# Differential attention in a hybrid layer: the turned output copied out of PSUM by VectorE and squared later by ScalarE, the last-but-one query group's small transfers on GpSimd's queue

## The chip, the cores and the metric

The kernel runs on one core of a Trainium2 chip. The metric is device time in microseconds (us) of one execution; lower is better. Before the change three runs took 2862.43, 2862.50 and 2864.21 us (median 2862.5 us).

## The reference, cut to what matters

One layer of a hybrid backbone: a combined input projection, differential attention with four heads beside a Fourier mix, an output projection of both, and a squared-ReLU MLP. The attention is where the change lies. Each head has two score maps (m = 0, 1), and their softmaxes are subtracted; each head's output is then normalised over its 128 values:

```python
def one_block(qblk):
    s = jnp.einsum('bqhmd,bkhmd->bhmqk', qblk, k).astype(jnp.float32) * scale
    p = jax.nn.softmax(s, axis=-1)
    a = p[:, :, 0] - lam * p[:, :, 1]
    return jnp.einsum('bhqk,bkhe->bqhe', a.astype(v.dtype), v)

def merge(attn, four, subln_g, lam_init, w_out):
    b, n = attn.shape[:2]
    a = rms_norm(attn, subln_g) * (1.0 - lam_init)
    return jnp.concatenate([a.reshape(b, n, ATTN_WIDTH), four], axis=-1) @ w_out
```

There are 2048 latent queries against 2560 keys (512 cached, 2048 latent), and 256 prompt queries against the prompt's own 256 keys.

## The kernel before

**Engines.** PE is TensorE, PEld its weight load, DVE VectorE, ACT ScalarE, POOL GpSimd, SP SyncE. Each works through its own instructions in the order in which they were written; an instruction that waits for another engine or a DMA holds up what is behind it.

**Stages.** Up to 517 us run the projections and the Fourier mix, which ends with four stores of ys to the array four by GpSimd's queue (L830). From 517 to 1250 us comes attention, then the out-projection, then the MLP, which TensorE fills to the end.

**Attention.** Each of four heads has eight groups of 256 queries (class Group), taken one after the other, and one prompt group. A group's steps are methods: fill (TensorE: scores S of 128 queries and 512 keys into a PSUM bank, two products, L1081), rowmax and comb (VectorE: the row's maximum, L1086 and L1089), exp (ScalarE: L1105, into P0 for m = 0 and P1 for m = 1, with the row sums), combine (VectorE sums, L1110 and L1111; GpSimd scales P1 and adds it to P0, L1112 to L1121), tr (TensorE turns P0 into pt, L1136), ah and al (ScalarE copies pt as the high part, VectorE takes the remainder, L1143 and L1148), mul (TensorE: values times probabilities into po, L95 to L97 for the split blocks, L1162 for blocks 4 and 14, which are kept whole in the tile af).

**The group's output.** po is one PSUM bank for all groups. Its columns 0 to 255 take the product; o1 copies them to oT (ScalarE, L1173), o2 turns oT with TensorE into po's columns 256 to 511 (L1177), o4 squares these with a sum over each row (ScalarE, two ACTIVATE into the scratch tile osq, L1183), o5 turns the sums into factors (GpSimd, L1186 and pow at L92), o6 stores the factors (DMA rs, L1194), o7 loads them back spread over the partitions (DMA rb, L1199), o8 multiplies oT by them (GpSimd, L1204), and o9 stores the result (DMA att, L1208). place says which queue o6, o7 and o9 use: SyncE's, or GpSimd's for the last group of the last head ("last", group 7). The one before it, group 6 of the last head, is "drain".

**What sets the order.** Every step is entered with a hand-written time by add(t, fn), in units of u = 1.04, the steps are sorted by these times and written out in that order. The last group's steps from o4 on are put aside (LASTO) and run inside the out-projection, the first two behind its first six products, the others behind its first twelve.

**The step into the out-projection.** The out-projection takes token tiles s0, s1 and so on. w_split makes high and low parts of the weights (woh on ScalarE, wol on VectorE, L1561 to L1565), mix those of the mixed activations (mh and ml on VectorE, L1588 and L1589, from mT), out_mm multiplies (L95 to L97), out_post adds to the residual (L1607, L1608), x_norm and finish feed the MLP. mix_load brings mT from att and four by SyncE's queue (L1581, L1582). In attention's pools tiles are laid out one behind the other in SBUF in the order of the pools: a_t (small tiles, ah, al, af, P1, and the output's tiles oT, osq, oss), then a_p (P0). They lie on memory that the stage before has given back.

Of the kernel before, what the change touches and what calls it, by code (L numbers as in the profile page):

```python
# [11 lines left out]
F32 = mybir.dt.float32  # L12
F32R = mybir.dt.float32r
AF = mybir.ActivationFunctionType
# [5 lines left out]
P = 128  # L20
# [21 lines left out]
def body(tc, a, out):  # L42
    nc = tc.nc
    ctx = ExitStack()
    with ctx:
# [944 lines left out]
        with ExitStack() as c3_:  # L990
# [4 lines left out]
            at = c3_.enter_context(tc.tile_pool(name="a_t", bufs=2, reuse_waits="tile"))  # L995
# [44 lines left out]
            class Group:  # L1040
# [97 lines left out]

                def ah(self, kb):
                    full = kb in self.hd.vf  # L1140
                    t = at.tile([P, 512], F32 if full else F32R, tag="af" if full else "ah", name=f"ah{self.nm}_{kb}", bufs=2 if full else 4)

                    (nc.vector.tensor_copy if self.drain and kb == FULL[0] else nc.scalar.copy)(t, self.pt[kb])  # L1143
                    self.A[kb] = [t]
# [30 lines left out]
                def o2(self):  # L1175
                    for j in range(2):
                        nc.tensor.transpose(self.po[:, 256 + j * P:256 + j * P + P], self.oT[:, j * P:j * P + P], ident)  # L1177

                def o4(self):
                    osq = self.op.tile([P, P], F32, tag="osq", name=f"osq{self.nm}", bufs=1)  # L1180
                    self.oss = self.op.tile([P, 4], F32, tag="oss", name=f"oss{self.nm}")
                    for j in range(2):
                        nc.scalar.activation(osq, self.po[:, 256 + j * P:256 + j * P + P], AF.Square, accum_out=self.oss[:, j:j + 1])  # L1183

                def o5(self):
                    nc.gpsimd.tensor_add(self.oss[:, 0:2], self.oss[:, 0:2], self.s0e)  # L1186
                    pow_mhalf(self.oss[:, 2:4], self.oss[:, 0:2], 2)

                def place(self):
                    return nc.gpsimd if self.last else nc.sync, self.hd.tok0 // 2 + self.g  # L1190

                def o6(self):
                    q, n = self.place()
# [16 lines left out]
            class Prompt(Group):  # L1210
# [39 lines left out]
                def mul(self):  # L1250

                    (ah, al), V = self.A[0], self.hd.V
                    for t in range(2):
                        c = slice(t * 256, t * 256 + 256)
                        for n, (l, r) in enumerate(((0, ah), (1, ah), (0, al))):
                            nc.tensor.matmul(PRO()[:, 256:512], V[:, t, l, :], r[:, c], start=False, stop=(t == 1 and n == 2), skip_group_check=True)
# [23 lines left out]
            def add(t, fn, *args):  # L1280
                ev.append((t, len(ev), fn, args))
# [20 lines left out]
            for h in range(H):  # L1302
                hd, hp = Head(0, h), Head(1, h)
                base = h * 32 * T
                add(base - 18 * T + 0.7 if h else -3.04 * T, hd.load_k)
                add(base - 14 * T + 0.7 if h else 0.9 * T, hd.load_v)
                e = 4 * T * (h == H - 1)
                add(base + 2 * T - e + 0.7, hp.load_k)
                add(base + 2 * T - e + 0.71, hp.load_v)
                gp = Prompt(hp, 0)  # L1310
                G = [base + (AVS + 4 * g) * T for g in range(8)]
                add(G[1] - 3 * T - e, gp.qload)
                for j in range(2):
                    for m in range(2):
                        for t, fn in ((0.4, gp.scores), (0.85, gp.rowmax), (2.7, gp.exp)):
                            add(G[1 + 2 * j + m] - e + t * u, fn, j, m)
                    add(G[2 + 2 * j] - e + 8 * u, gp.combine, j)
                for t, fn, *args in ((0.25, gp.tr, 0), (0.9, gp.ah), (1.4, gp.al), (17.0, gp.mul), (20.85, gp.o1), (24.45, gp.oq),
                                     (25.3, gp.o2), (26.0, gp.o5), (26.05, gp.opow), (29.5, gp.o6), (34.0, gp.o7),
                                     (40.2, gp.o8), (43.0, gp.o9)):  # L1320
                    add(G[5] - e + t * u, fn, *args)
                for g in range(hd.ng):
                    gr = Group(hd, g)
                    add(base - (4 if h or g > 1 else 3) * T + 0.6 * u if base else -3.03 * T, gr.qload)
                    for st in range(4):
                        j, m = divmod(st, 2)
                        t0 = base + st * T
                        for b in range(hd.nbk):
                            add(t0 - T + (0.76 + 0.66 * b) * u, gr.fill, j, m, b)
                            add(t0 - T + (1.26 + 0.66 * b) * u, gr.rowmax, j, m, b)  # L1330
                            add(t0 + 0.66 * b * u, gr.exp, j, m, b)
                        add(t0 - 0.45 * u, gr.comb, j, m)
                        if m:
                            add(t0 + (4.5 if gr.last and j else 5.9) * u, gr.combine, j)
                            if gr.last and j:
                                add(t0 + T + 5.3 * u, gr.combine_v, j)
                    kbs = list(range(0, hd.nkt, 2))
                    for q in range(4):
                        w = base + (AVS + q) * T
                        if q % 2 == 0:  # L1340
                            order = [kbs.pop(0) for _ in range(2)]
                            tr_t, ah_t, al_t = [0.7, 2.2], [3.3, 3.8], [4.6, 5.2]
                        else:
                            order = [kbs.pop(0) for _ in range(3)]
                            tr_t, ah_t, al_t = [0.7, 2.2, 3.86], [3.3, 3.8, 4.4], [None, 4.6, 5.2]
                        for n, kb in enumerate(order):
                            add(w + tr_t[n] * u, gr.tr, kb)
                            add(w + (2.0 if gr.drain and kb == FULL[0] else ah_t[n]) * u, gr.ah, kb)
                            if al_t[n]:
                                add(w + al_t[n] * u, gr.al, kb)  # L1350
                            add(w + T + (3.9 + 0.01 * n) * u, gr.mul, kb)
                            if q == 3 and not n:
                                add(w + 3.95 * u, gr.mul_part, kb)
                    w = base + (AVS + 5) * T + 1.0 * u
                    for t, fn in ((0, gr.o1), (0.4, gr.o2), (6.9, gr.o4), (9.2, gr.o5), (11.8, gr.o6), (16.3, gr.o7), (23.4, gr.o8), (26.0, gr.o9)):
                        if gr.last and t > 1:
                            LASTO.append(fn)
                        else:
                            add(w + t * u, fn)
                    base += 4 * T  # L1360
# [357 lines left out]
        with c5r, ExitStack() as c5:  # L1718
# [157 lines left out]
            with tc.manual_schedule():  # L1876
                for n, (q, p) in enumerate(ITEMS):
# [22 lines left out]
                    fn, args = FINISH.get(n, (None, ()))  # L1900
# [66 lines left out]
        with ExitStack() as c6:  # L1967
# [62 lines left out]
            with tc.manual_schedule():  # L2030
                pend, NM, loaded, KS = None, 7 * 24, 4, []
                for i in range(7):
                    for b in range(3):
                        ps = [pp.tile([P, 512], F32, tag="ps", name=f"ps{i}_{b}_{j}", bufs=6) for j in range(3)]
                        for k in range(16):
# [19 lines left out]
                            if (i, b) == (6, 2) and 9 <= k < 12:  # L2055

                                j = k - 9
# [14 lines left out]
                for j in range(3):  # L2072
                    t = 6 + j
# [70 lines left out]
```

## Time and profile before

| | us |
|---|---|
| median of 3 runs | 2862.5 |
| the profiled execution | 2864.23 |
| its span, first to last instruction | 2862.4 |
| PE busy | 2829.3 (99%) |
| DVE busy | 1978.0 (69%) |
| ACT busy | 1534.8 (54%) |
| POOL busy | 1075.4 (38%) |

The page's chain of work that ended last gives PE 54% of the span by name and DVE 1%. In rows of instructions the columns are start, duration, engine, line, operation, output and inputs, shapes and count, and in brackets the idle time ahead of it on its engine and what ended it. In rows of waits they are the total, the count and the longest.

### The profile page before, as it was taken

How to read it: one execution, taken by the hardware profiler on the slowest of the kernel's cores; microseconds unless marked ns; L12 is line 12 of the kernel's file. 1: busy time of each engine (PE TensorE's matmuls, PEld its weight loads, DVE VectorE, ACT ScalarE, POOL GpSimd, SP SyncE). 2: the span in 40 equal slices, each digit the busy share in tenths (PEclk: the TensorE clock that was granted, in tenths of full speed). 3: DMA queues.
4: the chain of work that ended last, by engine and by line, in shares of the span. 5: the costliest groups of instructions: out<-in, count | busy, mean ns of one | idle time of the engine just before them, and what ended most of it. 6: DMA issues, size and time to landing. Idle time of an engine off the chain costs nothing.

```text
span 2862.4 us, 42998 instructions
## 1 busy us (share of the span) xinstructions
PE 2829.3 (99%) x15029; PEld 2453.4 (86%) x15029; DVE 1978.0 (69%) x3325; ACT 1534.8 (54%) x3479; POOL 1075.4 (38%) x887
## 2 busy tenths in 40 slices
PE   8999999999999999999999999999999999999999
PEld 5888888688888888878889999999998888888887
DVE  7777786888888888864477777778775354345554
ACT  4333332798988989853356565556555332333221
POOL 1221223789999899942223333333332000000000
PEclk9999999999999999999999999999999999999999
DMA  7777767432222322246767676667747464445653
GB/s 284 219 209 204 234 203 253 153 105 54 78 74 53 112 62 75 50 120 210 247 221 232 221 247 229 220 220 238 233 168 256 147 202 136 137 143 185 208 203 111
DMA packets 404795, 497.69 MB, mean 174 GB/s; under 512 B 31539, under 2 KB 320672, under 8 KB 401506
## 3 DMA queue, kind: packets, MB, share of 16 engines
q1 hardware_dynamic: 399088, 484.35, 53.5%
q0 software_dynamic: 1936, 7.41, 0.8%
q10 hardware_dynamic: 3554, 3.17, 0.4%
q8 instruction: 119, 1.95, 0.3%
q14 instruction: 98, 0.80, 0.1%
HBM read 317.30 MB, written 179.62 MB: 174 GB/s over the span
## 4 chain that ended last, share of the span: by engine, by line
PE 54%; DVE 1%; DMA 0%; issue 0%; ACT 0%; POOL 0%; DVEq 0%; SPq 0%
PE ps L95 8%; PE ps L96 8%; PE ps L97 8%; PE pB L1761 2%; PE pB L1759 2%; PE pB L1760 2%; PE pA L1759 2%; PE pA L1761 2%; PE pA L1760 2%; PE pC L1761 2%; PE pC L1759 2%; PE pC L1760 2%; PE po L97 2%; PE po L96 2%; PE po L95 2%; PE pD L1759 1%
## 5 line engine op out<-in xcount | busy, mean ns | idle before, releaser
L1086 DVE TENSOR_REDUCE mxs<-Ss 128x1 f32<-128x512 f32 x636 | 405.4, 686 | 98.5 <-PE Ss L1081 91.2
L1436 DVE TENSOR_TENSOR sl<-sr,sh 128x768 fp32r<-128x768 f32 x168 | 161.8, 964 | 331.6 <-ACT sh L1435 331.1
L1121 POOL TENSOR_TENSOR P0s<-P0s,P1s 128x1024 f32<-128x1024 f32 (+2 forms) x128 | 378.5, 2957 | 10.7
L1435 ACT CAST sh<-sr 128x768 fp32r<-128x768 f32 x168 | 140.6, 838 | 418.3 <-PE ps L96 418.3
L1801 POOL TENSOR_TENSOR gs<-g,g 128x384 f32<-128x384 f32 x48 | 69.8, 1453 | 469.3 <-ACT g L1771 426.4
L1105 ACT ACTIVATE P1s<-Ss,mxs 128x512 f32<-128x512 f32 x318 | 215.2, 694 | 38.8 <-DVE mxs L1089 35.4
L95 PE MATMUL pj<-wh,hh 128*128 128x512 f32 x576 | 228.2, 396 | 2.0 <-DVE hh L556 2.0
L95 PE MATMUL ps<-thT,sh 128*128 128x512 f32 x585 | 227.6, 389 | 0.0
L96 PE MATMUL ps<-tlT,sh 128*128 128x512 f32 x585 | 227.6, 389 | 0.0
L97 PE MATMUL ps<-thT,sl 128*128 128x512 f32 x585 | 227.6, 389 | 0.0
L96 PE MATMUL pj<-wl,hh 128*128 128x512 f32 x576 | 227.0, 394 | 0.3 <-DVE wl L517 0.3
L97 PE MATMUL pj<-wh,hl 128*128 128x512 f32 x576 | 225.4, 392 | 0.0
L1105 ACT ACTIVATE P0s<-Ss,mxs 128x512 f32<-128x512 f32 x318 | 214.4, 691 | 4.9 <-DVE mxs L1089 4.0
L1136 PE MATMUL pts<-ident,P0s 128*128 128x128 f32 x1280 | 192.5, 274 | 4.5 <-DVE als L1148 1.8
L1081 PE MATMUL Ss<-KS0s,Qs 128*128 128x512 f32 x636 | 190.6, 420 | 0.4 <-ACT P1s L1105 0.4
L1081 PE MATMUL Ss<-KS1s,Qs 128*128 128x512 f32 x636 | 189.1, 422 | 1.5 <-ACT P0s L1105 1.1
L1136 PEld LDWEIGHTS pts<-ident,P0s 128*128 128x128 f32 x1280 | 152.5, 141 | 35.7 <-issue 4.6
L1770 ACT ACTIVATE g<-uz 128x384 f32<-128x384 f32 x144 | 75.7, 526 | 200.1 <-DVE uz L1793 174.0
L1120 POOL TENSOR_SCALAR P1s<-P1s,tots 128x1024 f32<-128x1024 f32 (+2 forms) x128 | 171.6, 1340 | 5.8
L1148 DVE TENSOR_TENSOR als<-pts,ahs 128x512 fp32r<-128x512 f32 x256 | 163.7, 681 | 9.4 <-ACT ahs L1143 9.3
L95 PE MATMUL ps<-ophT,sh 128*128 128x512 f32 x423 | 164.7, 389 | 1.1 <-DVE uz L1793 1.1
L1143 ACT CAST ahs<-pts 128x512 fp32r<-128x512 f32 x256 | 146.8, 604 | 34.1 <-PE pts L1136 34.1
(534 smaller groups left out, 8021.0 us busy)
## 6 DMA issues: line engine op xcount, KB each, us to landing
sr<-sd SPq DMA_DIRECT2D x84, 768.0 KB, 4.4
a<-in_w SPq DMA_DIRECT2D x184, 256.0 KB, 3.6
sd<-gs SPq DMA_DIRECT2D x192, 192.0 KB, 2.0
sd<-g SPq DMA_DIRECT2D x144, 192.0 KB, 4.1
wm<-in_w_mod SPq DMA_DIRECT2D x32, 512.0 KB, 5.3
Qs<-qd SPq DMA_DIRECT2D x32, 512.0 KB, 5.3
b<-in_w SPq DMA_DIRECT2D x64, 256.0 KB, 5.0
b<-tsum SPq DMA_DIRECT2D x64, 256.0 KB, 4.7
```

The source lines that it names most:

```text
L95: nc.tensor.matmul(ps, lh, rh, start=first, stop=False)
L96: nc.tensor.matmul(ps, lh, rl, start=False, stop=False)
L97: nc.tensor.matmul(ps, ll, rh, start=False, stop=last)
L1081: nc.tensor.matmul(S[:, :w], self.Q[:, x, m, j * P:j * P + P], self.hd.KS[m][:, b * 512:b * 512 + w], start=(x == 0), stop=(x == 1))
L1086: nc.vector.tensor_reduce(self.mx[j][:, m, b:b + 1], self.S[j, m, b], axis=AX.X, op=ALU.max)
L1105: nc.scalar.activation(dst, S, AF.Exp, bias=self.mx[j][:, m, 6:7], accum_out=self.sm[j][:, m, b:b + 1])
L1120: nc.gpsimd.tensor_scalar(p, p, tot[:, 3:4], 0.0, op0=ALU.mult, op1=ALU.add)
L1121: nc.gpsimd.tensor_add(d, d, p)
L1136: nc.tensor.transpose(pt[:, c:c + P], self.p0[j][:, (kb + t) * P:(kb + t + 1) * P], ident)
L1759: nc.tensor.matmul(ps, wh[:, c], hh[:, k, :], start=first and k == 0, stop=False, skip_group_check=True)
L1760: nc.tensor.matmul(ps, wh[:, c], hl[:, k, :], start=False, stop=False, skip_group_check=True)
L1761: nc.tensor.matmul(ps, wl[:, c], hh[:, k, :], start=False, stop=k == 3, skip_group_check=True)
```

## The change

1. A new step o3 copies the turned output, 128x256, from po to a new SBUF tile o on VectorE, at 4.25 u behind o1 (0.75 u for the last group). 2. o4 squares o in place instead of reading po, and goes from 6.9 u to 8.5 u; the scratch tile osq (128 wide) is gone, o is 256 wide. 3. af has one buffer instead of two. 4. The last-but-one group's o6, o7 and o9 go to GpSimd's queue.

```diff
-   t = at.tile([P, 512], F32 if full else F32R, tag="af" if full else "ah", name=f"ah{self.nm}_{kb}", bufs=2 if full else 4)
+   t = at.tile([P, 512], F32 if full else F32R, tag="af" if full else "ah", name=f"ah{self.nm}_{kb}", bufs=1 if full else 4)
...
+   def o3(self):
+       self.o = self.op.tile([P, 256], F32, tag="o", name=f"o{self.nm}", bufs=1)
+       nc.vector.tensor_copy(self.o, self.po[:, 256:512])
+
    def o4(self):
-       osq = self.op.tile([P, P], F32, tag="osq", name=f"osq{self.nm}", bufs=1)
        self.oss = self.op.tile([P, 4], F32, tag="oss", name=f"oss{self.nm}")
        for j in range(2):
-           nc.scalar.activation(osq, self.po[:, 256 + j * P:256 + j * P + P], AF.Square, accum_out=self.oss[:, j:j + 1])
+           o = self.o[:, j * P:j * P + P]
+           nc.scalar.activation(o, o, AF.Square, accum_out=self.oss[:, j:j + 1])
...
-       return nc.gpsimd if self.last else nc.sync, self.hd.tok0 // 2 + self.g
+       return nc.gpsimd if self.last or self.drain else nc.sync, self.hd.tok0 // 2 + self.g
...
-   for t, fn in ((0, gr.o1), (0.4, gr.o2), (6.9, gr.o4), (9.2, gr.o5), (11.8, gr.o6), (16.3, gr.o7), (23.4, gr.o8), (26.0, gr.o9)):
+   for t, fn in ((0, gr.o1), (0.4, gr.o2), (0.75 if gr.last else 4.25, gr.o3), (8.5, gr.o4), (9.2, gr.o5), (11.8, gr.o6), (16.3, gr.o7), (23.4, gr.o8), (26.0, gr.o9)):
```

**Place 1, the start of attention.** ScalarE's first exponentials, in the brackets what each waits for (a name without DMA is an engine, DMASW0 to 7 are the counters that GpSimd's DMAs raise in turn); before:

```order
L811 COPY abl_0_5199<-pabl_0_5196 128x130 [waits PE_49]
L811 COPY abl_1_5204<-pabl_1_5201 128x130 [waits PE_49,Activation_49]
L760 COPY yu<-py 128x129 [waits PE_49] x2
L1105 ACTIVATE P0s_0_0_5289,sms_0_0_5266<-Ss_0_0_0_0_5268,mxs_0_0_5265 128x512 [waits DVE_49,Pool_49]
L1105 ACTIVATE P0s_0_0_5289,sms_0_0_5266<-Ss_0_0_0_1_5272,mxs_0_0_5265 128x512
```

and now:

```order
L811 COPY abl_0_5199<-pabl_0_5196 128x130 [waits PE_49]
L811 COPY abl_1_5204<-pabl_1_5201 128x130 [waits PE_49,Activation_49]
L760 COPY yu<-py 128x129 [waits PE_49] x2
L1105 ACTIVATE P0s_0_0_5289,sms_0_0_5266<-Ss_0_0_0_0_5268,mxs_0_0_5265 128x512 [waits DMASW0_49,DVE_49,Pool_49]
L1105 ACTIVATE P0s_0_0_5289,sms_0_0_5266<-Ss_0_0_0_1_5272,mxs_0_0_5265 128x512
```

The first exponential has got a wait for DMASW0. GpSimd's last DMAs ahead of it are the stores of ys, in both kernels; each waits for the counter that it will raise:

```order
L779 TENSOR_TENSOR ys_4700<-yu 128x256
L830 DMA four<-ys_4697 128x2048 [waits DMASW5_49,DVE_49]
L830 DMA four<-ys_4698 128x2048 [waits DMASW6_49,DVE_49]
L830 DMA four<-ys_4699 128x2048 [waits DMASW7_49,DVE_49]
L830 DMA four<-ys_4700 128x2048 [waits DMASW0_49,DVE_49,Pool_49]
```

The count that the exponential waits for is the one that the fourth of these, ys_4700, raises when it has landed.

**Place 2, a group in the middle of attention.** ScalarE, group 3 of the first head (P0s and P1s are group 6's probabilities, ahs_4 group 4's), before:

```order
L1105 ACTIVATE P0s_6_0_6803,sms_6_0_6736<-Ss_6_0_0_4_6774,mxs_6_0_6735 128x512
L1183 ACTIVATE osqs_3_6848,osss_3_6849<-po 128x128 [waits DMAHW6_49,PE_49]
L1183 ACTIVATE osqs_3_6848,osss_3_6849<-po 128x128 [waits Activation_49]
L1143 CAST ahs_4_10_6853<-pts_4_10_6811 128x512 [waits PE_49]
L1143 CAST ahs_4_12_6858<-pts_4_12_6838 128x512 [waits PE_49]
```

and now:

```order
L1105 ACTIVATE P0s_6_0_6806,sms_6_0_6739<-Ss_6_0_0_4_6777,mxs_6_0_6738 128x512
L1143 CAST ahs_4_10_6854<-pts_4_10_6816 128x512 [waits PE_49,Activation_49]
L1143 CAST ahs_4_12_6859<-pts_4_12_6843 128x512 [waits PE_49,Activation_49]
L1187 ACTIVATE os_3_6810,osss_3_6876<-os_3_6810 128x128 [waits DMAHW6_49,DVE_49]
L1187 ACTIVATE os_3_6810,osss_3_6876<-os_3_6810 128x128
```

The two squares have gone behind the two copies and wait for VectorE. VectorE has the copy between the remainders and the sums:

```order
L1148 TENSOR_TENSOR als_4_6_6804<-pts_4_6_6759,ahs_4_6_6780 128x512 [waits Activation_49]
L1148 TENSOR_TENSOR als_4_8_6808<-pts_4_8_6782,ahs_4_8_6800 128x512 [waits Activation_49]
L1181 COPY os_3_6810<-po 128x256 [waits PE_49]
L1110 TENSOR_REDUCE tots_5_1_6596<-sms_5_1_6595 128x2 [waits Pool_49]
L1111 RECIPROCAL tots_5_1_6596<-tots_5_1_6596 128x1 [waits DVE_49]
L1086 TENSOR_REDUCE mxs_6_0_6738<-Ss_6_0_1_0_6821 128x1 [waits PE_49]
```

TensorE's order is the same in both; its first product of group 4, `L1162 MATMUL po<-ahs_4_4`, waits for VectorE where it waited for ScalarE.

**Place 3, the end of attention.** VectorE's last remainders and the out-projection's first splits, before:

```order
L1148 TENSOR_TENSOR als_7_16_14805<-pts_7_16_14775,ahs_7_16_14783 128x512 [waits Activation_49]
L1148 TENSOR_TENSOR als_7_18_14807<-pts_7_18_14785,ahs_7_18_14803 128x512 [waits Activation_49]
L1562 SCALAR_TENSOR_TENSOR wol_0_14890<-wout_13384,cols,woh_0_14882 128x512 [waits DMAHW6_49,Activation_49,Pool_49]
L1588 CAST mh_14911<-wout_13386 128x1024 [waits DMAHW2_49,DMAHW3_49,DMASW4_49,DMAHW6_49,DMASW3_49,DMAHW7_49,DMASW2_49,DMASW1_49]
L1589 TENSOR_TENSOR ml_14912<-wout_13386,mh_14911 128x1024 [waits DMAHW3_49,DVE_49]
```

and now (os_7 is the last group's copy, the lines are 4 higher):

```order
L1148 TENSOR_TENSOR als_7_16_14836<-pts_7_16_14806,ahs_7_16_14814 128x512 [waits DVE_49,Activation_49]
L1148 TENSOR_TENSOR als_7_18_14838<-pts_7_18_14816,ahs_7_18_14834 128x512 [waits DVE_49,Activation_49]
L1181 COPY os_7_14860<-po 128x256 [waits PE_49,Activation_49]
L1566 SCALAR_TENSOR_TENSOR wol_0_14923<-wout_13409,cols,woh_0_14915 128x512 [waits DMAHW6_49,Pool_49]
L1592 CAST mh_14944<-wout_13411 128x1024 [waits DMAHW2_49,DMAHW3_49,DMASW4_49,DMAHW6_49,DMASW3_49,DMAHW7_49,DMASW2_49,DMASW1_49]
L1593 TENSOR_TENSOR ml_14945<-wout_13411,mh_14944 128x1024 [waits DMAHW3_49,DVE_49]
```

The copy stands ahead of the three. GpSimd, the last two groups, now:

```order
L1198 DMA rs_84<-osss_6_14792 128x2 [waits DMASW1_49,Pool_49]
L1203 DMA rbs_6_14840<-rs_84 128x256 [waits DMASW2_49,DMASW1_49]
L1208 TENSOR_TENSOR oTs_6_14724<-oTs_6_14724,rbs_6_14840 128x256 [waits DMASW2_49,PE_49]
L1212 DMA att_79<-oTs_6_14724 128x256 [waits DMASW3_49,Pool_49]
L1190 TENSOR_TENSOR osss_7_14961<-osss_7_14961,s0es_7_14028 128x2 [waits Activation_49]
L92 TENSOR_TENSOR osss_7_14961<-osss_7_14961,mhalf 128x2 [waits Pool_49]
L1198 DMA rs_84<-osss_7_14961 128x2 [waits DMASW4_49,Pool_49]
L1203 DMA rbs_7_14981<-rs_84 128x256 [waits DMASW4_49]
L1208 TENSOR_TENSOR oTs_7_14856<-oTs_7_14856,rbs_7_14981 128x256 [waits DMASW5_49,PE_49]
```

The first, second and fourth rows stood on SyncE before, between the store of group 5's att and the load of mT.

## The prediction, as put on record

> **What bounds the kernel now.** I read the page's busy times first.
>
> ```profile
> PE 2829.3 (99%) x15029; PEld 2453.4 (86%) x15029; DVE 1978.0 (69%) x3325; ACT 1534.8 (54%) x3479; POOL 1075.4 (38%) x887
> ```
>
> TensorE is busy for 99% of the span, so an edit pays or costs only what it adds to or takes from TensorE's few stops. The change touches the attention stage alone (about 517 to 1250 us) and the step from it into the out-projection, so the second view is the table of waits from 560 to 1250 us.
>
> ```profile
> PEld Ss L1081 <- ACT P0s L1105: 14.9, 43, 0.5
> PEld po L1177 <- ACT oTs L1173: 12.0, 28, 0.7
> PEld po L1162 <- ACT osqs L1183: 10.1, 31, 0.3
> PEld Ss L1081 <- ACT P1s L1105: 5.2, 25, 0.2
> ```
>
> The third row is the one that the new copy addresses: 31 times the first value product of a group waits until ScalarE has squared the turned output of the group before, since both use the one PSUM tile po. PEld is only the weight load, though, which runs ahead of the products; 10.1 us is not yet TensorE's loss. The instruction rows tell what is. The first group has nothing to wait for, a later one has:
>
> ```profile
> 557.93 1.18 PE L1081 MATMUL Ss<-KS1s,Qs 128*128 128x512 f32 x4
> 558.94 1.03 PE L1162 MATMUL po<-ahs,vf4s 128*128 128x256 f32 x4
> 559.61 0.47 PE L95 MATMUL po<-ahs,Vs 128*128 128x256 f32 x1
> ...
> 715.27 1.17 PE L1081 MATMUL Ss<-KS1s,Qs 128*128 128x512 f32 x4
> 716.35 1.13 PE L1162 MATMUL po<-ahs,vf4s 128*128 128x256 f32 x4
> 717.13 0.47 PE L95 MATMUL po<-ahs,Vs 128*128 128x256 f32 x1
> ```
>
> From the four score products to the first L95 it is 559.61 − 557.93 = 1.68 us without the wait and 717.13 − 715.27 = 1.86 us with it. TensorE loses 0.18 us a group, about half of the row's 0.33 (10.1 / 31).
>
> **Term A, the copy and the later squares: −4.5 us.** If the wait went everywhere, 31 x 0.18 = 5.6 us would be won. What replaces it is VectorE's copy of 128x256 out of PSUM. The trace has no such copy; two rows lie on either side, a VectorE reduction that reads as much PSUM, and ScalarE's copy of that shape:
>
> ```profile
> L1225 DVE TENSOR_REDUCE tlp<-po x16: 424/424/425, 567.0 to 1149.5; 128x1 f32<-128x256 f32 x16
> ...
> 707.89 0.37 ACT L1173 COPY oTs<-po 128x256 f32<-128x256 f32 x1
> ```
>
> I take 0.42, VectorE's own. In the order it stands behind two remainders (als) and ahead of the sums, so in the group above here:
>
> ```profile
> 712.07 1.28 DVE L1148 TENSOR_TENSOR als<-pts,ahs 128x512 fp32r<-128x512 f32 x2
> 713.45 0.16 DVE L1111 RECIPROCAL tots<-tots 128x1 f32<-128x1 f32 x1
> 714.02 3.29 DVE L1086 TENSOR_REDUCE mxs<-Ss 128x1 f32<-128x512 f32 x5 [0.41 <-PE Ss L1081]
> ...
> 715.93 0.28 ACT L1183 ACTIVATE osqs<-po 128x128 f32<-128x128 f32 x1
> 716.10 0.20 ACT L1183 ACTIVATION_READ_ACCUMULATOR osqs<-po 128x1 f32 x1
> 717.60 0.69 ACT L1105 ACTIVATE P1s<-Ss,mxs 128x512 f32<-128x512 f32 x1 [0.34 <-DVE mxs L1089]
> ...
> 723.20 0.19 POOL L1186 TENSOR_TENSOR osss<-osss,s0es 128x2 f32<-128x2 f32 x1
> ```
>
> The copy runs from 713.35 to about 713.8, 2.5 us before the squares end now (716.30), so po is free in time and the wait goes. Its cover is the 0.41 us in which VectorE waits for scores: 0.42 fits in it almost exactly. What doesn't fit delays the row maxima, which then run without a gap, and with them the exponentials that already wait 0.34 for them; those free the banks that TensorE fills (the Ss rows above, 0.2 to 0.35 a time). Without that cover 30 groups would give back up to 0.18 each, and A would be 0. I charge 0.6 in all for it, and 0.5 at the last-but-one group, whose copy has remainders ahead of it longer than the squares took: 5.6 − 0.6 − 0.5 = 4.5. Bounds: 0 to −5.6. The squares (0.28 each) stay on ScalarE; from SBUF the trace has none, and I take the same length: were they twice as long, ScalarE would lose 0.6 us a group against the 0.34 that it waits there, which is the second rival's case. Moved behind two copies of probabilities they end about a microsecond later, at 717.4, and GpSimd comes to them at 723.20 only. One af buffer fewer is free: the product that uses it ends at 717.5 (716.35 + 1.13), and the next block's copy stands behind the exponentials that begin at 717.60.
>
> **Term B, the start of attention: +12.0 us.** Taking one af tile out and making o wider shortens the pool a_t by 2 − 0.5 = 1.5 KB a partition, and all that lies behind it moves down. The order of instructions shows what that does: the very first exponential, which before waits for VectorE and GpSimd, now waits for DMASW0 as well, the fourth of GpSimd's stores of the Fourier part (ys), whose tile lies where the probabilities now begin. When does that store land?
>
> ```profile
> 518.09 0.53 POOL L830 DMA_DIRECT2D four<-ys  x1 [0.35 <-issue]
> ...
> DMA to landing us min/median/max: 8.6/11.1/14.7
> ```
>
> ```profile
> 527.00:533.00 6.00, 5.70 (x18) 2.59 (x18) 5.57 (x14) 5.75 (x17) 4.61 (x5) 1.00 0.99 405
> 533.00:539.00 6.00, 5.72 (x18) 2.38 (x16) 5.56 (x13) 5.67 (x19) 5.74 (x5) 1.00 0.04 16
> ```
>
> The fourth store is issued at 518.09. In the windows (columns: PE, PEld, DVE, ACT and POOL busy, granted clock, share of the DMA engines) the DMA engines are full until about 533 and then empty, so the longest landing is the last one's: 518.09 + 14.7 = 532.8. Now the start as it is:
>
> ```profile
> 520.74 0.69 ACT L1105 ACTIVATE P0s<-Ss,mxs 128x512 f32<-128x512 f32 x1 [4.04 <-DVE mxs L1089]
> 521.57 1.40 PE L1081 MATMUL Ss<-KS1s,Qs 128*128 128x512 f32 x4 [1.10 <-ACT P0s L1105]
> 531.13 0.69 ACT L1105 ACTIVATE P1s<-po,mxs 128x512 f32<-128x512 f32 x1 [0.26 <-DVE mxs L1089]
> ```
>
> The first exponential runs at 520.74. TensorE has by then filled every bank and waits for it (1.10). From there to 545 ScalarE goes without a pause but for short ones like the 0.26 at 531.13, so it sets the pace and all behind it moves with it: 532.8 − 520.74 = 12.0. Two such pauses could be made up by maxima taken meanwhile (11.5). Were the fourth store as quick as the quickest, 518.09 + 8.6 = 526.7, it would be 6.0. Nothing hides any of it: there is no other work that TensorE could do there.
>
> By the Trainium skill (TensorE: Matmul & The Clock Gate, What's actually happening) an idle window of about 3.4 us halves TensorE's clock, and 12 us of idling would have TensorE refill the banks at half pace. This trace has that clock in one of the rows of the next part (0.50). ScalarE then has eight full banks to work off, so by that rule I'd add an estimated 0 to 1 us; I add nothing.
>
> **Term C, the step into the out-projection: −1.5 us.** Three DMAs of the last-but-one group go from SyncE's queue to GpSimd's, and the last group's copy stands on VectorE ahead of the weights' first split.
>
> ```profile
> 1245.40 1.32 DVE L1562 SCALAR_TENSOR_TENSOR wol<-wout,cols,woh 128x512 fp32r<-128x512 f32 x1
> 1247.36 1.23 DVE L1589 TENSOR_TENSOR ml<-wout,mh 128x1024 fp32r<-128x1024 f32 x1
> 1257.70 0.69 DVE L1588 CAST mh<-mT 128x1024 fp32r<-128x1024 f32 x1 [4.71 <-DMA mT<-att]
> ...
> 1248.01 0.44 PE L1177 MATMUL po<-ident,oTs 128*128 128x128 f32 x2 [0.46 <-ACT oTs L1173]
> 1258.54 0.47 PE L95 MATMUL po<-woh,mh 128*128 128x512 f32 x1 [4.39 <-DVE mh L1588]
> 1259.78 0.80 PE L97 MATMUL po<-woh,ml 128*128 128x512 f32 x1 [0.54 <-DVE ml L1589]
> ...
> 1246.20 0.32 SPq L1208 DMA_DIRECT2D att<-oTs  x1
> 1251.38 0.43 SPq L1581 DMA_DIRECT2D mT<-att  x1
> ...
> 1259.23:1262.64 3.41, 2.87 (x8) 2.29 (x8) 3.41 (x6) 0.00 (x0) 0.16 (x1) 0.50 1.02 351
> ```
>
> Now TensorE stops for 4.39 and 0.54 us and then runs 3.41 us at half clock, 1.7 lost: 6.6 in all. The cause is the load of mT, issued only at 1251.38 behind two DMAs of the last-but-one group. Without them it can go at about 1246.6 and lands, in the same 6.3 us, at 1252.9. But the last group's copy has to wait for the transposes (1248.01 + 0.44), ends at 1248.9, and wol, mh and ml follow in some 2.7 us instead of running from 1245.40 to 1248.6; the first L97 slides from 1248.75 to 1251.5, and the first block ends some 2.85 later. The second block's mh is ready at 1256.6, its ml at 1257.9: 3.3 us ahead of now (3.3 lost instead of 6.6). So half the gain is eaten by the new wait. From there GpSimd's chain takes back:
>
> ```profile
> 1258.72 0.67 POOL L1194 DMA_DIRECT2D rs<-osss  x1 [0.29 <-POOL osss L92]
> 1266.14 0.55 POOL L1199 DMA_DIRECT2D rbs<-rs  x1 [6.75 <-DMA rs<-osss]
> 1269.74 0.74 POOL L1204 TENSOR_TENSOR oTs<-oTs,rbs 128x256 f32<-128x256 f32 x1 [3.05 <-DMA rbs<-rs]
> 1276.47 0.57 POOL L92 TENSOR_TENSOR nrsb<-nssb,mhalf 128x1 f32<-128x1 f32 x1 [5.10 <-DVE nssb L230]
> ```
>
> Through this queue one group's factors take 6.75 + 3.05 us of waiting, and two groups' now stand in a row, from about 1248: the second ends at some 1272 to 1275, where GpSimd's pow for the norm of the stage's first tile, queued behind, is wanted near 1273 (1276.47 less 3.3). That takes up to 2.2 back, and the new 2.8 us stop can cost a half-clock window as above, 1.7. Bounds −3.3 to +0.6; I take −1.5.
>
> **Sum.** 12.0 − 4.5 − 1.5 = +6.0 us. The profiled execution took 2864.23 us (2862.4 of span); the three runs have a median of 2862.5, and I count from that: **2868.5 us**. A measurement of this kernel can tell some 0.2% (5.7 us) from no change, and +6.0 lies just outside.
>
> **Rivals.**
> - *The start isn't late* (faster). The store lands before the exponential needs it, or ScalarE's wait is satisfied early; then only A and C stay, −6.0: 2856.5 us. For it: the landing is an inference from a longest value. Against: the DMA engines are full until 533. It decides where the landing falls below 520.7. With the landing at 526.7 the change comes out even, 2862.5. Together 0.14.
> - *The copy is in the way* (slower still). The 0.42 us don't fit the 0.41 gap, the maxima go late, and A is 0; C as taken: +10.5, 2873 us. It decides where VectorE's gap is under the copy's length in most groups. For it: the Ss rows show ScalarE close behind TensorE. Against: TensorE's own gain shifts the copy too. Chance 0.2.
> - *GpSimd's queue takes all of C*: −4.5 + 12 + 0.6 = +8.1, 2870.6 us. Chance 0.13. The Trainium skill has a rule for it (SBUF — State Buffer, "DVE blocks DMA" trap): a DMA from GpSimd's queue can't get its descriptors written while VectorE copies in fp32 between SBUF tiles. By it three more DMAs could each wait out one cast like mh, at most an estimated 2.1 us; the trace shows only that the rs store at 1258.72 begins after the cast of 1257.70.
> - *The copy doesn't free po*: L1162 still waits. The order of instructions shows a wait for VectorE in the place of ScalarE's, so 0.03; then +10.5.
>
> **Chances.** The forecast itself has 0.5; the bounds of A and C move it by about ±3, so half of it lies above +5.7. Slower: 0.24 of the forecast, 0.17 of the late copy, 0.09 of the queue and 0.02 of the last rival, 0.52. Faster: 0.1, all from the first rival (its 0.14 less the even case). Same: what is left, 0.38. The likeliest case's own range is 2865.5 to 2871.5; with the late copy (2873) and the even case (2862.5) inside, 8 in 10 lie in 2860 to 2874.
>
> **What would show it.** B: the first L1105 at about 532.8 with a wait for a DMA of four, and TensorE idle some 12 us ahead of it. A: the row of L1162 waiting for osqs gone, with no new row of L1162 and no growth of the Ss rows beyond a few us. C: mT issued near 1246.6 (plus the shift), TensorE's stop of 4.39 replaced by one of about 2.8 earlier and one below 1. It is wrong if the first exponential runs near 520.7, or if the Ss waits grow by what L1162's lose.

## The result, and the profile after

| | before | changed |
|---|---|---|
| median of 17 runs each, us | 2863.21 | 2868.98 |
| lowest to highest | 2862.43 to 2865.81 | 2867.37 to 2872.68 |
| span of the profiled execution | 2862.4 | 2867.9 |

The ratio is 1.0021, with a 95% interval of 1.0013 to 1.0028: 5.8 us slower, where 6.0 had been forecast. The start of attention comes first. These are ScalarE's first exponential, TensorE's first product behind it, the issue of the fourth ys store and the landing of all four; then two windows (PE, PEld, DVE, ACT and POOL busy, granted clock, DMA share, GB/s).

```profile
533.88 0.69 ACT L1105 ACTIVATE P0s<-Ss,mxs 128x512 f32<-128x512 f32 x1 [16.69 <-DMA four<-ys]
...
534.71 2.08 PE L1081 MATMUL Ss<-KS1s,Qs 128*128 128x512 f32 x4 [13.75 <-ACT P0s L1105]
```

```profile
518.57 0.53 POOL L830 DMA_DIRECT2D four<-ys  x1 [0.34 <-issue]
...
DMA to landing us min/median/max: 9.7/12.0/15.2
```

```profile
523.06:533.88 10.82, 0.00 (x0) 0.00 (x0) 0.00 (x0) 0.00 (x0) 0.00 (x0) 0.50 0.87 361
533.88:540.13 6.25, 5.42 (x13) 4.22 (x14) 3.59 (x6) 5.78 (x17) 0.00 (x0) 0.50 0.01 3
```

The wait for the store stands in the trace by name (518.57 + 15.2 = 533.8), and for 10.8 us no engine works. The second row shows that TensorE's clock is still halved 6.25 us into the work that follows. The waits of attention (572 to 1262 us) answer to those of before:

```profile
PEld Ss L1081 <- ACT P0s L1105: 14.8, 43, 0.5
PEld po L1177 <- ACT oTs L1173: 11.5, 28, 0.7
...
PEld Ss L1081 <- ACT P1s L1105: 7.5, 40, 0.2
...
PEld po L1162 <- DVE os L1181: 0.8, 1, 0.8
```

Of L1162's 31 waits one is left, the one at the last-but-one group. The Ss row of P1s has grown by 2.3 us of weight loads' time. In one of the groups in the middle, shown here, the copy fills VectorE's gap to the last tenth, and the maxima behind it start without a wait; over attention VectorE's waits for scores fall from 151 to 120:

```profile
723.44 0.41 DVE L1181 COPY os<-po 128x256 f32<-128x256 f32 x1
723.77 0.15 DVE L1110 TENSOR_REDUCE tots<-sms 128x2 f32<-128x10 f32 x1
723.96 0.17 DVE L1111 RECIPROCAL tots<-tots 128x1 f32<-128x1 f32 x1
724.20 3.29 DVE L1086 TENSOR_REDUCE mxs<-Ss 128x1 f32<-128x512 f32 x5
```

And the step into the out-projection:

```profile
1255.48 0.42 DVE L1181 COPY os<-po 128x256 f32<-128x256 f32 x1 [3.10 <-PE po L1177]
...
1257.32 0.77 PE L95 MATMUL po<-woh,mh 128*128 128x512 f32 x1 [1.94 <-DVE mh L1592]
...
1253.24 0.43 SPq L1585 DMA_DIRECT2D mT<-att  x1
...
1256.93:1263.76 6.83, 6.44 (x14) 4.59 (x15) 6.69 (x11) 6.30 (x12) 0.55 (x1) 0.50 0.96 268
...
1282.21 0.58 POOL L92 TENSOR_TENSOR nrsb<-nssb,mhalf 128x1 f32<-128x1 f32 x1 [3.84 <-DVE nssb L230]
```

The load of mT is issued 1.7 us ahead of the last transposes (now 1254.94), where it was 3.4 us behind them. The stop of 4.39 us is gone, a stop of 1.94 for mh stands earlier, and 6.83 us at half clock follow it. GpSimd waits 3.84 us for VectorE's sum: its chain was done in time.

From the start times of such rows I cut each trace into the same stretches: from the first score product to the first exponential (start), from there to the first output copy oT (ramp), from the first to the thirtieth oT (29 groups), on to the last oT (drain), and on to the last transpose of the out-projection's normalised tiles (step). What is left, the MLP, takes 1400.4 to 1400.8 us in all runs.

| us | start | ramp | 29 groups | drain | step | median against before, same chip |
|---|---|---|---|---|---|---|
| before, first profile | 4.19 | 51.87 | 650.98 | 24.00 | 214.17 | |
| before, again | 4.19 | 49.35 | 651.18 | 24.08 | 216.69 | |
| changed | 16.84 | 50.26 | 645.95 | 24.42 | 213.02 | +5.8 |
| padding | 4.19 | 49.35 | 646.36 | 24.41 | 214.91 | −7.0 |
| address alone | 17.01 | 49.97 | 650.34 | 23.92 | 215.86 | +13.2 |
| queue alone | 4.19 | 49.33 | 650.89 | 24.09 | 218.46 | +2.7 |
| copy alone | 4.19 | 49.33 | 646.75 | 24.36 | 213.25 | −6.7 |
| last group without copy | 4.20 | 49.41 | 646.91 | 24.43 | 220.57 | −0.4 |
| chain cut short | 4.21 | 49.39 | 647.00 | 25.73 | 208.74 | −11.3 |
| late squares | 4.17 | 49.40 | 696.47 | 23.70 | 213.72 | +41.0 |

### The profile page after: what moved, and what is told of

Read it like the earlier page. It is cut to its first block, busy times and chain, and to the rows that moved or that the text cites. A ratio compares the mean times of both kernels' runs of the same rounds, so it can differ in the third digit from the quotient of the medians.

```text
span 2867.9 us, 43210 instructions
## 1 busy us (share of the span) xinstructions
PE 2824.6 (98%) x15029; PEld 2455.1 (86%) x15029; DVE 1989.6 (69%) x3357; ACT 1533.1 (53%) x3479; POOL 1075.7 (38%) x890
## 3 DMA queue, kind: packets, MB, share of 16 engines
q10 hardware_dynamic: 3554, 3.17, 0.3%
## 4 chain that ended last, share of the span: by engine, by line
PE 53%; DVE 1%; DMA 0%; issue 0%; ACT 0%; SPq 0%; POOL 0%; DVEq 0%
PE ps L95 8%; PE ps L96 8%; PE ps L97 8%; PE pB L1765 2%; PE pB L1763 2%; PE pB L1764 2%; PE pA L1763 2%; PE pC L1763 2%; PE pC L1765 2%; PE pA L1764 2%; PE pC L1764 2%; PE pA L1765 2%; PE po L97 2%; PE po L96 2%; PE po L95 2%; PE pD L1765 1%
## 5 line engine op out<-in xcount | busy, mean ns | idle before, releaser
L97 PE MATMUL ps<-thT,sl 128*128 128x512 f32 x585 | 227.6, 389 | 0.0
L97 PE MATMUL pj<-wh,hl 128*128 128x512 f32 x576 | 225.8, 392 | 0.0
L96 PE MATMUL ps<-oplT,sh 128*128 128x512 f32 x423 | 164.6, 389 | 0.0
```

The source lines that it names most:

```text
L96: nc.tensor.matmul(ps, lh, rl, start=False, stop=False)
L97: nc.tensor.matmul(ps, ll, rh, start=False, stop=last)
```

## The experiments

Experiments 1 to 3 were measured on one chip and 4 to 7 on another, each beside the kernel before, whose medians there are 2864.52 and 2866.86 us. The expected times count from about 2863 us, so the differences are what to compare.

**1. Is it the address? Padding in, and the address alone.** The theory said that the late first exponential costs +12 and that without it the change would win; the rival, that the loss lies elsewhere. The padding moves the probabilities behind the last ys tile and leaves the rest of the change:

```diff
+            shift(at, 1024, "t")
```

> The changed kernel with 1 KB a partition put into attention's first pool, so that the probabilities begin behind the last ys tile again; the first exponential then has no wait for the store. Theory (three terms: start +12, copy -4.5, step -1.5): the start's loss goes and the rest stays, about -6 against before, 2857 us; the first exponential near 520.7, L1162's wait for squares still gone. Rival (the loss lies in the copy or in GpSimd's queue and the late start is made up later): within 2 us of the changed kernel, 2867 to 2871.

Measured: 2857.51 us against 2864.52 (ratio 0.9977, 0.9967 to 0.9986). The other way round, the kernel before gets the changed kernel's addresses and nothing else:

```diff
+            shift(at, 512, "t")
...
-   ... tag="af" if full else "ah", name=f"ah{self.nm}_{kb}", bufs=2 if full else 4)
+   ... tag="af" if full else "ah", name=f"ah{self.nm}_{kb}", bufs=1 if full else 4)
```

> The kernel before with one af buffer and 0.5 KB of padding, so that the probabilities begin at the same address as in the changed kernel; nothing else of the change. Theory: only the start's loss, +11 to +12, 2874 to 2875 us, first exponential near 533, and all other waits as before. Rival (the start's idle time is made up behind it): under +3.

Measured: 2877.7 us against 2864.52 (1.0046, 1.0034 to 1.0059). The first exponentials of the two:

```profile
521.48 0.69 ACT L1106 ACTIVATE P0s<-Ss,mxs 128x512 f32<-128x512 f32 x1 [4.04 <-DVE mxs L1090]
```

```profile
535.13 0.69 ACT L1106 ACTIVATE P0s<-Ss,mxs 128x512 f32<-128x512 f32 x1 [16.86 <-DMA four<-ys]
```

With the padding the wait is for the row maxima, as before the change; with the address alone it is for the store. The two agree on the price: 13.2 us by the second, 5.8 + 7.0 = 12.8 by the first. The second is 1.2 more than was expected; its trace has 12.8 of it in the start and 0.6 in the ramp. The rivals fall: the start's loss is neither made up later nor a part of something else. One buffer of af makes no difference that shows: the 29 groups of the address alone take 650.34.

**2. The queue alone.** Undoing nothing, I gave the kernel before just the other queue:

```diff
-                    return nc.gpsimd if self.last else nc.sync, self.hd.tok0 // 2 + self.g
+                    return nc.gpsimd if self.last or self.drain else nc.sync, self.hd.tok0 // 2 + self.g
```

> The kernel before with the last-but-one group's three DMAs on GpSimd's queue and nothing else. Theory: mT is issued some 4.8 us earlier and without the last group's copy on VectorE TensorE's stop of 4.39 us goes almost whole; GpSimd's longer chain takes 1 to 3 back: -3 to -5, 2858 to 2860. Rival (GpSimd's chain of two groups decides, each DMA held up): 0 to +2.

Measured: 2867.21 us against 2864.52 (1.0008, 0.9999 to 1.0017). The theory falls here, and the rival is the nearer. TensorE's stop for mT did go, but GpSimd's chain then decided. GpSimd's rows, VectorE's and TensorE's:

```profile
1246.83 0.66 POOL L1194 DMA_DIRECT2D rs<-osss  x1 [0.29 <-POOL osss L92]
1254.40 0.55 POOL L1199 DMA_DIRECT2D rbs<-rs  x1 [6.92 <-DMA rs<-osss]
1262.54 0.74 POOL L1204 TENSOR_TENSOR oTs<-oTs,rbs 128x256 f32<-128x256 f32 x1 [7.58 <-DMA rbs<-rs]
...
1278.18 0.58 POOL L92 TENSOR_TENSOR nrsb<-nssb,mhalf 128x1 f32<-128x1 f32 x1
...
1278.79 0.75 DVE L236 TENSOR_SCALAR xn<-xo,nrsb 128x1024 f32<-128x1024 f32 x1 [9.91 <-POOL nrsb L92]
...
1279.60 1.97 PE L249 MATMUL ptb<-ident,xn 128*128 128x128 f32 x8 [9.81 <-DVE xn L236]
```

Two groups' factors one behind the other keep GpSimd from 1246.83 to 1278.15, 31.3 us, against the 24 to 27 (1248 to 1272 or 1275) that I had put down. The norm of the first tile waits 9.91 us for its pow, TensorE 9.81, and runs at half clock afterwards.

**3. The copy alone.** The padding, the copy and the later squares, the old queue:

```diff
+            shift(at, 1024, "t")
...
-                    return nc.gpsimd if self.last or self.drain else nc.sync, self.hd.tok0 // 2 + self.g
+                    return nc.gpsimd if self.last else nc.sync, self.hd.tok0 // 2 + self.g
```

> The changed kernel with the padding and with the last-but-one group's DMAs on SyncE's queue as before: the copy and the later squares alone. Theory: 30 waits of L1162 at 0.17 us won, 0.5 lost at the last-but-one group, the last group's copy hidden in TensorE's stop for mT: -4 to -5, 2858 to 2859. Rival (the copy doesn't fit VectorE's gap): 0 or above, 2863 to 2865.

Measured: 2857.81 us against 2864.52 (0.9976, 0.9967 to 0.9985). The 29 groups take 646.75 us, 4.2 to 4.4 less than before, and the rival falls. The whole is some 2 us better than expected; that lies in the step, 213.25 against 214.17 and 216.69. TensorE's stops there:

```profile
1244.59 0.47 PE L95 MATMUL po<-woh,mh 128*128 128x512 f32 x1 [1.94 <-DVE mh L1593]
...
1253.98 0.50 PE L97 MATMUL po<-woh,ml 128*128 128x512 f32 x1 [0.54 <-DVE ml L1594]
```

The copy's stop of 1.94 and a window of 3.41 us at half clock (from 1246.90) lie in the first block, ahead of the place where TensorE waited 4.39 and 0.54 for mT; 0.54 of that wait is left, and before the change the window lay behind it. So the copy alone takes most of the stop for mT with the old queue; this is read from one trace. Against experiment 1's padded kernel the queue is worth nothing (2857.51 and 2857.81).

**4. The last group without the copy.** If the last group's copy costs 2.8 us on VectorE, leaving it out should pay; if GpSimd's chain is what waits behind, it should cost. The padded kernel (here with 1.5 KB), with the last group's squares on PSUM as before:

```diff
+            shift(at, 1536, "t")
...
                 def o3(self):
+                    if self.last:
+                        self.o = self.po[:, 256:512]
+                        return
...
+                    osq = self.op.tile([P, P], F32, tag="osq", ...) if self.last else None
...
-                        nc.scalar.activation(o, o, AF.Square, accum_out=self.oss[:, j:j + 1])
+                        nc.scalar.activation(osq if self.last else o, o, AF.Square, accum_out=self.oss[:, j:j + 1])
```

> The changed kernel with padding (no wait at the start), and the last group without the copy: its squares read PSUM as before, so nothing stands ahead of the weights' split on VectorE; both last groups' DMAs stay on GpSimd's queue. Theory (GpSimd's chain of two groups, some 30 us long, ends later than the norm of the first tile needs it once TensorE isn't held up): TensorE's stop at the step goes, and a new one of 5 to 9 us ahead of the first L249 comes, as in the run with the queue alone: copy's -4.5 and the queue's +2.7, 2861 to 2864 us, slower than with the last group's copy. Rival (the last group's copy costs its 2.8 us whole): 2 to 3 faster than with it, 2854 to 2856.

Measured: 2866.47 us against 2866.86 (0.9997, 0.9988 to 1.0006), near the theory's −1.8, and 6.6 us worse than with the copy (−0.4 against −7.0); the rival falls. The stop ahead of the first L249 is longer than the 5 to 9 us that were expected. Its step (GpSimd, TensorE, VectorE), and behind it GpSimd's add and TensorE in the padded kernel of experiment 1:

```profile
1243.42 1.17 POOL L1195 TENSOR_TENSOR osss<-osss,s0es 128x2 f32<-128x2 f32 x1
1244.67 1.08 POOL L92 TENSOR_TENSOR osss<-osss,mhalf 128x2 f32<-128x2 f32 x1
...
1276.81 0.58 POOL L92 TENSOR_TENSOR nrsb<-nssb,mhalf 128x1 f32<-128x1 f32 x1
...
1278.24 1.97 PE L249 MATMUL ptb<-ident,xn 128*128 128x128 f32 x8 [11.14 <-DVE xn L236]
...
1242.89 1.65 DVE L1598 TENSOR_TENSOR ml<-wout,mh 128x1024 fp32r<-128x1024 f32 x1
```

```profile
1240.34 0.19 POOL L1191 TENSOR_TENSOR osss<-osss,s0es 128x2 f32<-128x2 f32 x1
1240.60 0.69 POOL L92 TENSOR_TENSOR osss<-osss,mhalf 128x2 f32<-128x2 f32 x1
...
1251.93 0.50 PE L97 MATMUL po<-woh,ml 128*128 128x512 f32 x1 [0.41 <-DVE ml L1594]
...
1271.05 1.97 PE L249 MATMUL ptb<-ident,xn 128*128 128x128 f32 x8 [2.95 <-DVE xn L236]
```

Where VectorE waits for the last group's transposes GpSimd's add takes 0.19 us; where it splits the weights at the same time the add takes 1.17 and the split's ml 1.65 instead of 1.23. The multiply ahead of the add and the pow behind it take longer as well, 1.12 for 0.74 and 1.08 for 0.69. So the factors of the last-but-one group are sent off 1.9 us behind the last transposes (1246.05 and 1244.15) instead of 0.4 ahead of them (1241.59 and 1242.03): of these 2.3 us the three longer operations make 1.75. TensorE stops 11.14 us for the chain instead of 2.95. VectorE's wait for the pow is 7.7 us longer (10.71 and 3.00): 2.3 come from the later start, some 2.8 from a longer chain behind it, and some 2.6 from work that, without the copy, needs the pow sooner. What lengthens the chain behind its start is not shown.

**5. The chain cut short.** The run before, with the last group's factors worked out ahead of the wait for the group before, and its DMAs on SyncE's queue behind the next tile's loads:

```diff
-                    return nc.gpsimd if self.last or self.drain else nc.sync, self.hd.tok0 // 2 + self.g
+                    return nc.gpsimd if self.drain else nc.sync, self.hd.tok0 // 2 + self.g
...
-   (8.5, gr.o4), (9.2, gr.o5),
+   (0.8 if gr.last else 8.5, gr.o4), (0.9 if gr.last else 9.2, gr.o5),
...
                 out_mm(s0, 1, 0, 2)
-                for fn in LASTO[:2]:
-                    fn()
                 w_split(1, 4)
                 out_mm(s0, 1, 2, 4)
-                for fn in LASTO[2:]:
+                mix_load(s2)
+                x_load(s2)
+                for fn in LASTO:
                     fn()
...
-                mix_load(s2)
-                x_load(s2)
```

> As the run before, and GpSimd's chain cut short: the last group's factors are worked out ahead of the wait for the group before, and its three DMAs go through SyncE's queue behind the loads of the next tile's activations. Theory: no stop at the start, no stop for mT, no stop ahead of L249: -4.5 for the copy and -4 to -6 for the step, 2853 to 2856 us, below all others. Rival (the stop moves to another wait of the step): within 1.5 us of the padded kernel, 2856 to 2859.

Measured: 2855.56 us against 2866.86 (0.9957, 0.9943 to 0.9971), 11.3 us faster than before. It is the best of all, as the theory says; the rival falls. Its step takes 208.74 us, 5.4 to 8.0 less than before, though 1.3 us have only moved into the drain, which takes 25.73 instead of 24.43. TensorE's wait ahead of the first L249 is 0.60, as in the kernel before (0.59). The edit moves three things at once (the last group's factors, the queue of its DMAs, the next tile's loads); which of them the gain needs is not shown. What remains of stops there is one on ScalarE, which has got the weights' casts ahead of the last output's copy:

```profile
1244.64 0.44 PE L1178 MATMUL po<-ident,oTs 128*128 128x128 f32 x2 [1.91 <-ACT oTs L1174]
```

**6. The squares later, without a copy.** To lengthen the wait that the copy takes away:

```diff
-   ... (6.9, gr.o4), ...
+   ... (8.5, gr.o4), ...
```

> The kernel before with the squares at 8.5 u, behind the two copies of probabilities, and still reading PSUM: the wait that the copy removes, made longer. Theory: the squares hold po, so L1162's wait grows by the 1.06 us of the two copies in some 30 groups, +25 to +35 us, 2888 to 2899 us, and the row of L1162 waiting for osqs grows to about 40 us. Rival (po is held by something else, or TensorE's time there is covered): within 3 us of before.

Measured: 2907.89 us against 2866.86 (1.0138, 1.0125 to 1.0152), more than expected, and not through the row that was named. The waits from 571 to 1295 us:

```profile
PEld Ss L1081 <- ACT P1s L1105: 63.9, 108, 1.4
ACT osqs L1183 <- PE po L97: 54.9, 26, 2.2
...
PE Ss L1081 <- ACT P1s L1105: 31.8, 29, 1.1
```

L1162 no longer waits for the squares; the squares wait for L97. At 8.5 u they come behind the next group's first products, so ScalarE stands still up to 2.2 us a group until these are done with po; as I read the rows, its exponentials then go late, and TensorE waits for the banks. The theory's mechanism is not tested by this. What it shows is another thing: later squares are to be had only with the copy.

**7. The kernel before, again.** 

> The kernel before, unchanged, for a second profile. Theory: the half-clock windows at 542 and 549 us of its first profile are a matter of where TensorE's stops of 1.4 and 1.9 us fall in the windows; the time from the first exponential to the first output may be 2.5 us shorter, as in the run with the queue alone. Rival: the same windows again, the same 51.9 us.

Nothing is edited; its one run took 2865.44 us. The ramp took 49.35 us instead of 51.87, as expected, and the step 216.69 instead of 214.17. In the ramp the windows of the half clock account for it: in the first profile 542.43 to 545.85 and 549.26 to 552.67, in the second none there.

```profile
542.43:545.85 3.42, 3.42 (x13) 2.71 (x12) 2.04 (x3) 3.11 (x9) 3.34 (x2) 0.50 0.00 0
549.26:552.67 3.41, 3.41 (x13) 2.73 (x12) 2.03 (x3) 2.76 (x9) 3.41 (x2) 0.50 0.08 28
```

```profile
535.00:552.67 17.67, 13.78 (x59) 8.16 (x60) 14.59 (x31) 16.06 (x46) 17.00 (x12) 1.00 0.09 32
1257.73:1264.56 6.83, 5.28 (x12) 3.73 (x13) 6.06 (x9) 0.00 (x0) 1.98 (x3) 0.50 1.04 350
...
1259.23 0.77 PE L95 MATMUL po<-woh,mh 128*128 128x512 f32 x1 [6.43 <-DVE mh L1588]
```

In the step two things come together: the half clock lasts 6.83 us instead of 3.41, and TensorE's stop for mT is 6.43 us instead of 4.39 and 0.54, since mT is issued 4.8 us behind the last transposes and not 3.4. So a stretch of one profile carries some 2.5 us of chance, in the ramp from where the windows fall, in the step from mT's time as well, and a term of that size can't be read from one pair of profiles.

## Why the prediction was right, step by step

- **The sum.** +6.0 forecast, +5.8 measured. In the traces, against the second profile of before, it is 12.65 (start) + 0.91 (ramp) − 5.23 (groups) + 0.34 (drain) − 3.67 (step) − 0.26 (MLP) − 0.46 (all ahead of attention, in which the programs don't differ) = +4.3; against the first profile 12.65 − 1.61 − 5.03 + 0.42 − 1.15 − 0.28 + 0.49 = +5.5. Both ways the start outweighs the rest. That the sum came within 0.2 us is in part luck: against the second profile the start and the ramp cost 1.6 us more than forecast, the copy and the step won 2.6 more, and these partly cancel.
- **B, the start: right, and sized 0.7 too small.** 12.65 for 12.0. The last store took 15.2 us to land, not 14.7; it was issued half a microsecond later in that execution (518.57), but so was the first score product. The idle time cost more on top: the ramp takes 50.26 us, and 49.97 in the address alone, instead of 49.3 to 49.4 in the runs that come out of the start at full clock and keep it. This fits the half clock for which I added nothing: TensorE's first four products behind the exponential take 2.08 us instead of 1.40. By the rule of the Trainium skill (TensorE: Matmul & The Clock Gate, What's actually happening) my estimate was 0 to 1, and the trace has 0.6 to 0.9.
- **A, the copy: right.** Its price of 0.42 us was 0.41 to 0.42, the gap took it, and the 29 groups became 5.0 to 5.2 us shorter in the changed kernel, 4.0 to 4.8 in the four other runs with the copy, where 5.0 stood (5.6 less 0.6). The 0.5 at the last-but-one group is 0.3 to 0.4. The squares from SBUF, taken as long as those from PSUM, were longer, 0.34 us against 0.28 (medians), but far from the twice as long that the second rival needed. That TensorE loses only half of the weight load's row was the step on which "slower" hung: with 10.1 us from that row the sum would have come to +1.5, too little to tell from no change.
- **C, the step: the size within chance, its make-up not right.** −1.5 forecast; −1.15 or −3.67 by the profile of before, whose stop for mT is 4.39 in one and 6.43 in the other. That −1.15 lies near −1.5 is luck. The stop of 2.8 us measured 1.94. The half clock that I charged as one window of 1.7 at most came as two windows, 6.83 us. The first block ran mostly at that pace, and the second block's mh and ml, ready when I had put them, weren't waited for; in the padded kernel, whose first block runs at full clock, TensorE waits 0.41 for that ml.
- **GpSimd's queue** was the weakest step. I let its chain take back "up to 2.2" and gave the queue's rival 0.13. In the changed kernel it takes nothing, and in the padded one, where TensorE stops 2.95 us ahead of the first L249 (0.59 before), some 2.4; alone it turns the expected gain of 3 to 5 into no gain (+2.7, 0.9999 to 1.0017), and without the last group's copy it costs 6.6 against the padded kernel. What had failed is that I added the terms: TensorE's delay by the copy and GpSimd's chain run beside each other, and the longer one counts. The copy, which looked like a cost there, hid most of the chain and let GpSimd start 2.3 us sooner against the last transposes.
- **The rivals.** The start that isn't late is out by experiment 1, the copy in the way by experiment 3, po that isn't freed by the row of L1162. The rule of the Trainium skill on DMAs from GpSimd's queue (SBUF — State Buffer, "DVE blocks DMA" trap) is not settled by any run here. In the padded kernel a cast of 0.69 us falls into the wait behind the second group's store, with the DMA engines empty; that wait is 3.17 us where the changed kernel, without a cast there, has 3.01, but the cast begins 2.1 us behind the issue.

## What to carry to other kernels

A buffer that is made smaller moves every tile behind it, and the first tile of a stage can come to lie on memory that a slow store of the stage before is still reading; the list of waits of the first instructions shows it ahead of any run, and 1 KB of padding took the 12.8 us away. A wait of the weight load is not TensorE's loss: compare the time between products with the wait and without. And a stop at a change of stage has other chains behind it: before it is removed, find the one that is next, since removing it alone can pay nothing (the step takes 218.46 us with the queue alone, 208.74 without the last copy and with the chain behind it shortened too).

## What the hardware showed that I had not expected

- GpSimd's add of 128x2 took 0.19 us beside an idle VectorE and 1.17 us beside a VectorE instruction with two SBUF inputs, which itself took 1.65 us instead of 1.23; GpSimd's multiply was still running when that one began. The Trainium skill (SBUF — State Buffer, SBUF: two separate sides) states that the two share a pair of ports by an exclusive lock, against VectorE instructions of this kind too; these rows agree with it.
- Inside these traces the half clock stays in steps of 3.41 us: 3.41, 6.83, 10.24, 13.65 and 17.07 us. It came after stops of 1.36 and 1.85 us in one profile of before and not in the other, so a stop shorter than a window can bring it.
- A store of 128x2 factors through GpSimd's queue kept the next issue waiting for 4.73 us in the changed kernel and 6.92 in the queue alone while the DMA engines were full (shares of 0.99 and 1.02), and the second group's for 3.01 in the changed kernel with the engines empty (0.01). In the queue alone the second group's took 4.95 with a share of 0.75, though VectorE was busy for only 0.15 us of it. In these rows the time of a small transfer goes with what else the DMA engines carry.
